# A sparse layer's rotated queries: transposed by TensorE, or by VectorE and a trip through memory

## The chip, the cores and the metric

The kernel runs on one core of a Trainium2 chip. The metric is device time in microseconds (us). Three runs of the kernel before took 723.4, 724.43 and 725.69 us; the median, 724.43 us, is the time before.

## The reference, cut to what matters

The model is a chain of layers over 256 positions of 1024 features, in float32: feed-forward, a mixer, feed-forward, a "forgetting" attention (fox) and a sparse attention (dsa), with the last two followed by a layer norm. The change lies in dsa:

```python
q, ckv, kr, qi, ki, wi, gate = split(x @ w_in)
q = rope(q.reshape(B, S, 8, 128))          # the first 32 of 128 are rotated
q_lat = einsum('bshn,hcn->bshc', q[..., 32:], w_uk)
q_full = concat([q_lat, q[..., :32]])
...                                        # an index picks 64 keys per query
logits = einsum('bqhc,bqkc->bhqk', q_full, selected) * 128 ** -0.5
o = softmax(logits) @ selected[..., :128] @ w_uv
out = (silu(gate) * o) @ w_out
```

## The kernel before, in words

The 256 positions are two tiles of 128, t = 0 and 1. A projection is computed in blocks: for one tile and 512 columns of weights, four units of two 128-row slices. Each float32 weight block is loaded on SyncE's queue (L210), rounded to a high part on ScalarE (`whi`, L197), and its remainder taken on VectorE (`wlo`, L198). Three fp32r matmuls per slice (L164) make one float32 product, so a block of 512 columns is 24 matmuls. `prefetch` runs up to eight units ahead.

In dsa the order of work is: an index block for each tile (`idx`, `idx_T`, `index`, `add`, with the top-k selection on VectorE at L991 and L992), then q in two halves j of four heads, each for t = 0 and 1, then the gate blocks (`attend`: two for tile 0, two for tile 1), between which the scores, softmax, products and `uv` of six groups of heads run, then the output projection (`out_proj`).

For one q block, `q_evac` copies the product out of PSUM on ScalarE (`yq`, L1016) and rotates it with six VectorE instructions (L920 to L925). `go` transposes its four heads on TensorE with the identity (`tr`, L179), copies the result scaled to `qT` (L1024), and puts the 32 rotated rows into `qs`, a stack of high part, remainder and high part again (L1026 to L1028). When both tiles of a half are there, `q_lat` multiplies by `w_uk` (two heads a call), and ScalarE and VectorE evacuate it. The scores use `qlT` and `qs`.

The order of the calls comes from a small planner. `self.now` is advanced by each matmul's planned time alone; `later(us, fn)` puts a call on a heap, due at `now + us`; `when` waits for named events first; `pump`, at the end of each unit, calls what is due; `drain` calls all that is left. The numbers are in `DUE`: `go` follows `q_evac` by `dsa_qT` = 6.31 us, and `q_lat` follows `go` of tile 1 by 1.0 and 2.0 us. This order is a rank and not yet the order on the engines: the framework that builds the program puts each engine's instructions into a fixed order by its own estimate of when inputs are there, and takes the earlier call where several could run. Each engine then runs its list strictly in that order and waits at each instruction for what it needs.

The feed-forward layers already have the other way to transpose: VectorE transposes 32x32 blocks of a 128x512 tile (`hb`, L413), and `regroup` (L275) moves the blocks to their partitions. It writes `hb` to a buffer in memory with four DMAs (L282, 128 KB each) and reads it back with one (L283, 512 KB), all on GpSimd's queue. Then `hh` (L239, ScalarE) and `hl` (L240, VectorE) split the landed `hd`, 9.5 us of planned time after the call.

Of the kernel before, what the change touches and what calls it, by code (L numbers as in the profile page):

```python
# [9 lines left out]
F32 = mybir.dt.float32  # L10
F32R = mybir.dt.float32r
BF16 = mybir.dt.bfloat16
AF = mybir.ActivationFunctionType
# [3 lines left out]
P = 128  # L17
S = 256
D = 1024
# [9 lines left out]
SC128 = 128 ** -0.5  # L29
# [17 lines left out]
def unit_list():  # L47
# [38 lines left out]
DUE = {  # L86
    "ffn_T": 9.5,
    "ffn_x": 3.0,
    "mix_T": 9.32,
    "mix_pool1": 1.21,  # L90
    "mix_pool2": 1.49,
    "mix_s": (0.5, 0.55, 3.0),
    "mix_pv": 1.0,
    "mix_pv2": 4.74,
# [5 lines left out]
    "out_T": 2.04,  # L100
    "dsa_idx": 3.93,
    "dsa_isc": (4.17, 0.39, 10.61),
    "dsa_qT": 6.31,
    "dsa_ql": (1.0, 2.0),
    "dsa_pv2": 1.64,
    "dsa_uv": 10.62,
# [8 lines left out]
class Kern:  # L115
# [40 lines left out]

    def drain(self):
        while self.heap:
            due, _, fn = heapq.heappop(self.heap)
            self.now = max(self.now, due)  # L160
            fn()
# [495 lines left out]
    def silu_gate(self, pool, acc, out, hr):  # L657

        nc = self.nc
        th = pool.tile([P, 512], F32, name="th", bufs=2)  # L660
        nc.scalar.activation(th, acc, AF.Tanh, scale=0.5 if hr is None else hr)
        nc.vector.scalar_tensor_tensor(out, th, 1.0, acc, op0=ALU.add, op1=ALU.mult)

    def out_proj(self, u, after, last=False):

        for t in range(2):
            o = [self.bank("mm") for _ in range(2)]
            for n in range(2):
                if last and t == n == 1:
                    o = [o[0], o[1], self.bank("mm")]  # L670
                    for j, c in enumerate((slice(0, 256), slice(256, 512))):
                        for i in range(4):
                            self.half(o[1 + j], self.xT[t], u + 4 + i, i == 0, i == 3, cols=c)
                    continue
                for i in range(4):
                    self.half(o[n], self.xT[t], u + 4 * n + i, i == 0, i == 3)
                    if t == 1:
                        self.done(u + 4 * n + i + 1)
                    if t == 1 or i % 2:
                        self.prefetch(1)  # L680
            if t == 0:
                self.before_t1()
            after(t, o)
        return u + 8
# [185 lines left out]
    def gate_out(self, t, hb, o, l, f, gt):  # L870

        nc = self.nc
        ri = self.small("ri", 4, bufs=4)
        nc.vector.reciprocal(ri, l[:, 4 * hb:4 * hb + 4])
        nc.vector.tensor_scalar(ri, ri, f, None, op0=ALU.mult)
        for i in range(4):
            c = slice((4 * hb + i) * P, (4 * hb + i + 1) * P)
            nc.vector.scalar_tensor_tensor(gt[:, c], o[:, i * P:(i + 1) * P], ri[:, i:i + 1], gt[:, c],
                                           op0=ALU.mult, op1=ALU.mult)
        self.when([(self.stage, "open", t)], DUE["out_T"], lambda: self.put_T(  # L880
            self.xT[t], t, gt[:, 512 * hb:512 * hb + 512], 4 * hb, 4))


    def dsa(self, u, x_gain=None):
        self.stage = "dsa"
        nc, tc, A = self.nc, self.tc, self.A
        with tc.tile_pool(name="dsa", bufs=1, reuse_waits="tile") as pool:
# [5 lines left out]
            rope = pool.tile([P, 2, 96], F32, name="rope")  # L893
            nc.sync.dma_start(out=rope, in_=A["rope"])
            y = [pool.tile([P, 744], F32, name=f"y{t}", tag=f"A{t}") for t in range(2)]
            gt = [pool.tile([P, D], F32, name=f"g{t}") for t in range(2)]
            kiT, ckvT = (pool.tile([P, P], F32, name=n) for n in ("kiT", "ckvT"))
            qiT = pool.tile([P, 4, P], F32, name="qiT")
            kiTs, ckvTs = (self.parts(pool, [P, S], n) for n in ("kiTs", "ckvTs"))
# [3 lines left out]
            qs = pool.tile([96, 8, S], F32R, name="qs")  # L903
            ckvs = [tuple(pool.tile([P, P], F32R, name=f"ckv{c}{t}") for c in "hl") for t in range(2)]
            ckv = [pool.tile([P, P], F32, name=f"ckv{t}") for t in range(2)]
            qT = [pool.tile([P, 4, S], F32, name=f"qT{j}") for j in range(2)]
# [6 lines left out]
            def do_rope(x, n, half, t, off):  # L913

                x1, x2 = x[:, :, 0:half], x[:, :, half:2 * half]
                bc = lambda o: rope[:, t, None, off + o:off + o + half].to_broadcast([P, n, half])
                m = pool.tile([P, 2, 9 * 8], F32, name="rm", bufs=2)
                m1 = m[:, 0, :n * half].rearrange("p (n d) -> p n d", n=n)
                m2 = m[:, 1, :n * half].rearrange("p (n d) -> p n d", n=n)
                nc.vector.tensor_tensor(m1, x2, bc(half), op=ALU.mult)  # L920
                nc.vector.tensor_tensor(m2, x1, bc(half), op=ALU.mult)
                nc.vector.tensor_tensor(x1, x1, bc(0), op=ALU.mult)
                nc.vector.tensor_tensor(x2, x2, bc(0), op=ALU.mult)
                nc.vector.tensor_tensor(x1, x1, m1, op=ALU.subtract)
                nc.vector.tensor_tensor(x2, x2, m2, op=ALU.add)  # L925
# [88 lines left out]
            def q_evac(acc, t, j):  # L1014
                yq = pool.tile([P, 512], F32, name="yq", bufs=2)
                nc.scalar.copy(yq, acc)  # L1016
                do_rope(yq.rearrange("p (h d) -> p h d", h=4), 4, 16, t, 0)

                def go():
                    ps = self.bank("tr")  # L1020
                    for i in range(4):
                        self.tr(ps[:, i * P:(i + 1) * P], yq[:, i * P:(i + 1) * P])
                    hs, c = slice(4 * j, 4 * j + 4), slice(t * P, (t + 1) * P)
                    nc.scalar.activation(qT[j][:, :, c], ps.rearrange("p (i q) -> p i q", i=4), AF.Copy,  # L1024
                                         scale=SC128)
                    nc.scalar.copy(qs[0:32, hs, c], qT[j][0:32, :, c])  # L1026
                    nc.vector.tensor_sub(qs[32:64, hs, c], qT[j][0:32, :, c], qs[0:32, hs, c].bitcast(F32))
                    nc.scalar.copy(qs[64:96, hs, c], qs[0:32, hs, c].bitcast(F32))  # L1028
                    if t == 1:
                        for g in range(2):  # L1030
                            self.later(DUE["dsa_ql"][g], lambda g=g: q_lat(2 * j + g))
                self.later(DUE["dsa_qT"], go)

            def q_lat(g):
                ps = self.bank("sc").rearrange("p (h k) -> p h k", h=2)
                for i in range(2):
                    self.mm(ps[:, i, :], wuk[:, 2 * g + i, :], qT[g // 2][:, 2 * (g % 2) + i, :], True, True)
                nc.scalar.copy(qlT[:, 2 * g:2 * g + 2, :], ps[:, :, 0:P])
                self.split_psum(*(d[:, 2 * g:2 * g + 2, :] for d in qlTs), ps[:, :, P:S])
                self.fire(("dsa", "ql", g))  # L1040

            for j in range(2):
                for t, acc in self.chunk(u, 4):
                    q_evac(acc, t, j)
                u += 4
# [44 lines left out]
            for t, g in GROUPS:  # L1090
                ql = [("dsa", "ql", i) for i in ((2 * g, 2 * g + 1) if t == 0 else (g,))]
                self.when([("dsa", "sel", t)] + ql, 0.0, lambda t=t, g=g: self.fire(("dsa", "k", t, g)))
            self.attend(u, pool, gt, [None, None], scores, pv)
            u += 8
            rows = []
# [88 lines left out]
def layout(inp):  # L1184
# [7 lines left out]
        "fox": fox, "fox_fv": np.concatenate([fox[:, 3072:3080], fox[:, 2048:3072]], 1),  # L1192
        "fox_out": a["fox_w_out_2"],
        "dsa": dsa, "dsa_idx": np.concatenate([ki, qi, wi, kr, ckv], 1), "dsa_out": a["dsa_w_out_2"],
    }
    for i in (1, 2):
# [38 lines left out]
```

## Time and profile before

| | |
|---|---|
| median of three runs | 724.43 us |
| the profiled execution | 723.93 us, of which the span from first to last instruction is 722.1 |
| TensorE matmul busy | 706.5 us, 98% |
| VectorE busy | 492.1 us, 68% |
| ScalarE busy | 369.4 us, 51% |
| GpSimd busy | 62.3 us, 9% |
| mean granted TensorE clock | 0.993 of full speed |

Busy shares are averages over stages with different limits; the dsa layer begins at about 602 us of the span. Rows of a time line give start, duration, engine, line, operation with its tiles and shapes, a count, and in brackets the idle time of the engine just before and what ended it.

### The profile page before, as it was taken

The page shows a single profiled execution, that of the slowest core. Times are in us where ns is not written, and L with a number is a line of the kernel's source. Part 1 is how long each engine was busy: PE and PEld are TensorE (multiplying, and loading weights), DVE is VectorE, ACT ScalarE, POOL GpSimd, SP SyncE. Part 2 cuts the span into 40 slices and gives each one's busy share as a digit, 9 for nine tenths or more (in the row PEclk, how much of TensorE's full clock was granted, in tenths as well). Part 3 has the DMA queues.
Part 4 walks back from the last instruction along what each step waited for, and adds up shares of the span by engine and source line. Part 5 has one row for each costly group of instructions (what it writes and reads, how often), then busy time and mean ns, then how long its engine had stood idle before and what let it go on. Part 6 is the DMA issues. An engine that isn't in the chain of part 4 may idle for free.

```text
span 722.1 us, 9816 instructions
## 1 busy us (share of the span) xinstructions
PE 706.5 (98%) x3580; PEld 593.9 (82%) x3580; DVE 492.1 (68%) x790; ACT 369.4 (51%) x552; POOL 62.3 (9%) x90
## 2 busy tenths in 40 slices
PE   8999999999999999999999999999999999999995
PEld 7788889888888778888889888778898888778984
DVE  5776765575647867666776575556456968997965
ACT  6654544454545645454454354446464635675820
POOL 0101110300001001011110300000300001000001
PEclk9999999999999999999999999999999999999998
DMA  8898666875734425668765885546572527633501
GB/s 253 305 317 309 212 215 208 285 266 188 271 122 167 154 94 181 202 199 288 228 224 196 270 265 189 196 142 195 169 248 101 156 63 251 206 118 117 175 1 59
DMA packets 42305, 140.87 MB, mean 195 GB/s; under 512 B 5512, under 2 KB 6672, under 8 KB 42128
## 3 DMA queue, kind: packets, MB, share of 16 engines
q1 hardware_dynamic: 37728, 127.23, 52.7%
q0 software_dynamic: 4096, 12.60, 5.1%
q8 instruction: 28, 0.46, 0.2%
q10 hardware_dynamic: 432, 0.41, 0.2%
q14 instruction: 21, 0.17, 0.1%
HBM read 133.39 MB, written 6.82 MB: 194 GB/s over the span
## 4 chain that ended last, share of the span: by engine, by line
PE 88%; DVE 5%; DMA 3%; ACT 2%; issue 1%; SPq 0%; POOL 0%; DVEq 0%; POOLq 0%; ACTq 0%
PE mm L164 79%; PE sc L164 5%; PE tr L179 3%; DVE wlo L198 2%; DMA raw<-in_w 1%; DMA row_final_norm<-in_final_norm 1%; PE tr L164 1%; ACT whi L197 1%; DMA xin<-in_xT 1%; ACT s L445 0%; DVE sel L983 0%; DVE xl L317 0%; DVE sel L992 0%; DVE s L534 0%; POOL hrs L292 0%
## 5 line engine op out<-in xcount | busy, mean ns | idle before, releaser
L198 DVE TENSOR_TENSOR wlo<-raw,whi 128x1024 fp32r<-128x1024 f32 (+3 forms) x236 | 274.6, 1178 | 84.8 <-ACT whi L197 74.9
L197 ACT CAST whi<-raw 128x1024 fp32r<-128x1024 f32 (+3 forms) x236 | 235.7, 1014 | 126.0 <-PE mm L164 76.4
L164 PE MATMUL mm<-whi,xh 128*128 128x512 f32 (+3 forms) x760 | 289.3, 381 | 1.7 <-ACT whi L197 1.6
L164 PE MATMUL mm<-whi,xl 128*128 128x512 f32 (+3 forms) x760 | 284.9, 375 | 2.2 <-DVE xl L246 2.2
L164 PE MATMUL mm<-wlo,xh 128*128 128x512 f32 (+3 forms) x760 | 284.0, 375 | 0.1
L164 PEld LDWEIGHTS mm<-whi,xh 128*128 128x128 f32 x760 | 144.0, 189 | 25.7 <-ACT whi L197 3.0
L164 PEld LDWEIGHTS mm<-whi,xl 128*128 128x128 f32 x760 | 144.2, 190 | 25.0 <-DVE xl L246 2.7
L164 PEld LDWEIGHTS mm<-wlo,xh 128*128 128x128 f32 x760 | 143.9, 189 | 25.3 <-DVE wlo L198 1.3
L164 PE MATMUL mm<-whi,hh 128*128 128x512 f32 x176 | 68.7, 390 | 0.0
L164 PE MATMUL mm<-whi,hl 128*128 128x512 f32 x176 | 68.5, 389 | 0.0
L164 PE MATMUL mm<-wlo,hh 128*128 128x512 f32 x176 | 68.5, 389 | 0.0
L240 DVE TENSOR_TENSOR hl<-hd,hh 128x512 fp32r<-128x512 f32 (+1 forms) x24 | 14.5, 644 | 53.3 <-ACT hh L239 53.3
L239 ACT CAST hh<-hd 128x512 fp32r<-128x512 f32 (+1 forms) x24 | 12.8, 583 | 60.9 <-DMA hd<-d 60.9
L282 POOL DMA_DIRECT2D d<-hb x48 | 26.5, 559 | 149.9 <-DVE hb L413 136.3
L164 PEld LDWEIGHTS mm<-wlo,hh 128*128 128x128 f32 x176 | 33.0, 188 | 6.9
L164 PEld LDWEIGHTS mm<-whi,hh 128*128 128x128 f32 x176 | 33.1, 188 | 6.7
L164 PEld LDWEIGHTS mm<-whi,hl 128*128 128x128 f32 x176 | 33.1, 188 | 6.7
L400 ACT ACTIVATE th<-mm,hr 128x512 f32<-128x512 f32 (+1 forms) x24 | 15.6, 648 | 25.2 <-PE mm L164 24.1
L445 ACT ACTIVATE s<-s,nmax 128x128 f32<-128x128 f32 (+1 forms) x48 | 21.3, 446 | 7.0 <-DVE nmax L443 7.0
L292 POOL TENSOR_TENSOR rs<-ms,mhalf 128x1 f32<-128x1 f32 x10 | 6.5, 653 | 175.4 <-DVE ms L305 175.4
L402 DVE SCALAR_TENSOR_TENSOR a<-th,mm 128x512 f32<-128x512 f32 (+1 forms) x24 | 15.2, 632 | 8.5 <-ACT th L400 8.5
L292 POOL TENSOR_TENSOR lr<-ve,mhalf 128x1 f32<-128x1 f32 x4 | 4.0, 992 | 167.8 <-DVE ve L640 167.8
(219 smaller groups left out, 602.0 us busy)
## 6 DMA issues: line engine op xcount, KB each, us to landing
raw<-in_w SPq DMA_DIRECT2D x208, 512.0 KB, 4.5
d<-hb POOLq DMA_DIRECT2D x40, 128.0 KB, 4.8
hd<-d POOLq DMA_DIRECT2D x10, 512.0 KB, 6.6
raw<-in_w SPq DMA_DIRECT2D x12, 344.0 KB, 3.6
raw<-in_w SPq DMA_DIRECT2D x8, 372.0 KB, 3.6
raw<-in_w SPq DMA_DIRECT2D x8, 256.0 KB, 4.4
x<-in_x SPq DMA_DIRECT2D x2, 512.0 KB, 6.3
B<-in_bias SPq DMA_DIRECT2D x1, 1024.0 KB, 7.0
```

What stands on the lines that cost most here:

```text
L164: self.nc.tensor.matmul(out, a, b, start=start, stop=stop)
L179: self.nc.tensor.transpose(out, a, self.ident[:p, :p])
L197: nc.scalar.copy(hi[:, :m], raw[:, :m])
L198: nc.vector.tensor_sub(lo[:, :m], raw[:, :m], hi[:, :m].bitcast(F32))
L239: nc.scalar.copy(hi, src)
L240: nc.vector.tensor_sub(lo, src, hi.bitcast(F32))
L282: self.nc.gpsimd.dma_start(out=d[a].rearrange("b i m -> i b m"), in_=src[32 * a:32 * a + 32])
L292: self.nc.gpsimd.tensor_tensor(out, a, self.mhalf[:, 0:1].to_broadcast(list(a.shape)), op=ALU.pow)
L400: nc.scalar.activation(th[:, :w], acc[:, :w], AF.Tanh, scale=hr[t])
L402: nc.vector.scalar_tensor_tensor(a[t][:, :w], th[:, :w], 1.0, acc[:, :w], op0=ALU.add, op1=ALU.mult)
L445: nc.scalar.activation(s[:, h, :], s[:, h, :], AF.Exp, bias=m[:, h:h + 1], accum_out=l[:, col + h:col + h + 1])
```

## The change

The rotated q is no longer transposed by TensorE. VectorE transposes each rotated block in 32x32 blocks into `qb`; when both tiles of a half are in, `regroup` sends them through memory into `qd`. `go`, now once a half and due 9.0 us after the second tile, copies `qd` to `qT` and `qs` as before. `qb` has one buffer and shares it with the gate of tile 1 (`g1`, made later), and `th` of the gate shares the buffers of `yq`. `out_proj` first runs the planner until the transposes of the gated output of its tile have been called; this also holds for fox.

```diff
-    "dsa_qT": 6.31,
+    "dsa_qT": 9.0,
...
+    def until(self, keys):
+
+        while not all(k in self.fired for k in keys):
             due, _, fn = heapq.heappop(self.heap)
             self.now = max(self.now, due)
             fn()
...
-        th = pool.tile([P, 512], F32, name="th", bufs=2)
+        th = pool.tile([P, 512], F32, name="th", tag="yq" if self.stage == "dsa" else "th", bufs=2)
...
         for t in range(2):
+            self.until([(self.stage, "og", t, hb) for hb in range(2)])
             o = [self.bank("mm") for _ in range(2)]
...
-        self.when([(self.stage, "open", t)], DUE["out_T"], lambda: self.put_T(
-            self.xT[t], t, gt[:, 512 * hb:512 * hb + 512], 4 * hb, 4))
+
+        def go():
+            self.put_T(self.xT[t], t, gt[:, 512 * hb:512 * hb + 512], 4 * hb, 4)
+            self.fire((self.stage, "og", t, hb))
+        self.when([(self.stage, "open", t)], DUE["out_T"], go)
...
-            gt = [pool.tile([P, D], F32, name=f"g{t}") for t in range(2)]
+            gt = [pool.tile([P, D], F32, name=f"g{t}") for t in range(1)]
...
                 do_rope(yq.rearrange("p (h d) -> p h d", h=4), 4, 16, t, 0)
 
+                if t == 0:
+                    self.qb = pool.tile([P, 4, 256], F32, name="qb", tag="g1")
+                nc.vector.transpose(self.qb[:, :, t * P:(t + 1) * P].rearrange("p b (c j) -> p b c j", c=4),
+                                    yq.rearrange("p (c b j) -> p b c j", c=4, b=4))
+                if t == 0:
+                    return
+                qd = pool.tile([P, 4, 256], F32, name="qd")
+                self.regroup(qd, self.qb)
+
                 def go():
-                    ps = self.bank("tr")
-                    for i in range(4):
-                        self.tr(ps[:, i * P:(i + 1) * P], yq[:, i * P:(i + 1) * P])
-                    hs, c = slice(4 * j, 4 * j + 4), slice(t * P, (t + 1) * P)
-                    nc.scalar.activation(qT[j][:, :, c], ps.rearrange("p (i q) -> p i q", i=4), AF.Copy,
-                                         scale=SC128)
-                    ...
+                    hs = slice(4 * j, 4 * j + 4)
+                    for tt in range(2):
+                        c = slice(tt * P, (tt + 1) * P)
+                        nc.scalar.activation(qT[j][:, :, c].rearrange("p c (a j) -> p c a j", a=4),
+                                             qd[:, :, c].rearrange("p a (c j) -> p c a j", c=4), AF.Copy, scale=SC128)
+                        nc.scalar.copy(qs[0:32, hs, c], qT[j][0:32, :, c])
+                        nc.vector.tensor_sub(qs[32:64, hs, c], qT[j][0:32, :, c], qs[0:32, hs, c].bitcast(F32))
+                        nc.scalar.copy(qs[64:96, hs, c], qs[0:32, hs, c].bitcast(F32))
+                    for g in range(2):
+                        self.later(DUE["dsa_ql"][g], lambda g=g: q_lat(2 * j + g))
                 self.later(DUE["dsa_qT"], go)
...
+            gt.append(pool.tile([P, D], F32, name="g1", tag="g1"))
             self.attend(u, pool, gt, [None, None], scores, pv)
```

## Rows read from the trace of the kernel before

**Rows 1.** The page's chain that ended last, shares of the span by engine.
```profile
PE 88%; DVE 5%; DMA 3%; ACT 2%; issue 1%; SPq 0%; POOL 0%; DVEq 0%; POOLq 0%; ACTq 0%
```
**Rows 2.** The chain in order of time: start, us, what.
```profile
514.09 5.49 PE mm L164 x24
...
640.43 0.44 PE tr L179 x4
...
642.26 1.73 PE sc L164 x8
...
699.75 13.94 PE mm L164 x84
```
**Rows 3.** Stretches: length, busy us of PE, PEld, DVE, ACT, POOL, clock, DMA share, GB/s.
```profile
655.00:660.00 5.00, 5.00 (x33) 4.44 (x31) 4.93 (x14) 1.40 (x3) 0.00 (x0) 1.00 0.38 139
660.00:665.00 5.00, 5.00 (x32) 4.20 (x31) 2.85 (x7) 4.28 (x15) 0.00 (x0) 1.00 0.08 30
```
**Rows 4.** Time line of TensorE, the first transposes of yq.
```profile
633.84 0.63 PE L179 MATMUL tr<-cst,yq 128*128 128x128 f32 x4 [0.25 <-DVE yq L925]
```
**Rows 5.** Time line of VectorE in the feed-forward layers.
```profile
59.71 0.71 DVE L413 STREAM_TRANSPOSE hb<-h 128x512 f32<-128x512 f32 x1
...
73.74 1.30 DVE L240 TENSOR_TENSOR hl<-hd,hh 128x512 fp32r<-128x512 f32 x2 [6.19 <-ACT hh L239]
74.95 0.74 DVE L411 SCALAR_TENSOR_TENSOR h<-a,qr,mm 128x512 f32<-128x512 f32 x1
...
372.63 0.71 DVE L413 STREAM_TRANSPOSE hb<-h 128x512 f32<-128x512 f32 x1
```
**Rows 6.** Time line of GpSimd: a regroup of a feed-forward layer, and 704 us.
```profile
60.72 2.19 POOL L282 DMA_DIRECT2D d<-hb  x4 [17.25 <-DVE hb L413]
68.01 0.76 POOL L283 DMA_DIRECT2D hd<-d  x1 [5.10 <-DMA d<-hb]
...
704.45 0.99 POOL L292 TENSOR_TENSOR lr<-ve,mhalf 128x1 f32<-128x1 f32 x1 [76.01 <-DVE ve L640]
```
**Rows 7.** Time line of ScalarE in the feed-forward layers.
```profile
58.72 0.69 ACT L400 ACTIVATE th<-mm,hr 128x512 f32<-128x512 f32 x1 [0.81 <-PE mm L164]
...
73.08 1.14 ACT L239 CAST hh<-hd 128x512 fp32r<-128x512 f32 x2 [6.80 <-DMA hd<-d]
...
387.39 1.14 ACT L239 CAST hh<-hd 128x512 fp32r<-128x512 f32 x2 [7.44 <-DMA hd<-d]
```
**Rows 8.** Time line of VectorE: last instructions of three rotations, and a subtraction.
```profile
637.19 0.68 DVE L1027 TENSOR_TENSOR qs<-qT,qs 32x512 fp32r<-32x512 f32 x1
...
638.98 0.22 DVE L924 TENSOR_TENSOR yq<-yq,rm 128x64 f32<-128x64 f32 x1
...
645.93 0.22 DVE L925 TENSOR_TENSOR yq<-yq,rm 128x64 f32<-128x64 f32 x1
...
655.98 0.22 DVE L925 TENSOR_TENSOR yq<-yq,rm 128x64 f32<-128x64 f32 x1
```
**Rows 9.** Time line of ScalarE: the last q evacuation, and copies to qT and qs.
```profile
649.36 0.57 ACT L1016 COPY yq<-mm 128x512 f32<-128x512 f32 x1
...
657.18 0.60 ACT L1024 ACTIVATE qT<-tr 128x512 f32<-128x512 f32 x1 [2.51 <-PE tr L179]
657.81 0.62 ACT L1026 CAST qs<-qT 32x512 fp32r<-32x512 f32 x1
```
**Rows 10.** Time line of TensorE: transposes of two neighbouring calls of `idx_T`.
```profile
613.43 0.27 PE L179 MATMUL tr<-cst,ckv 128*128 128x128 f32 x1
...
615.57 0.28 PE L179 MATMUL tr<-cst,y 128*32 128x128 f32 x1
```
**Rows 11.** Time line of TensorE at the start of the fox layer.
```profile
470.49 0.80 PE L164 MATMUL mm<-whi,xl 128*128 128x512 f32 x1 [2.23 <-DVE xl L246]
```
**Rows 12.** Stretches of one microsecond behind that wait.
```profile
470.00:471.00 1.00, 0.52 (x1) 0.50 (x2) 1.00 (x2) 0.00 (x0) 0.00 (x0) 0.66 0.46 184
...
473.00:474.00 1.00, 1.00 (x4) 0.77 (x4) 1.00 (x3) 0.00 (x0) 0.00 (x0) 0.63 0.82 324
```

More of the change, by code (lines that the diff above doesn't have):

```diff
@@ L158, in drain @@
         while self.heap:
+            due, _, fn = heapq.heappop(self.heap)
+            self.now = max(self.now, due)
+            fn()
+    def until(self, keys):
+        while not all(k in self.fired for k in keys):
             due, _, fn = heapq.heappop(self.heap)
@@ L1017, in q_evac @@
                 do_rope(yq.rearrange("p (h d) -> p h d", h=4), 4, 16, t, 0)
-                def go():
-                    ps = self.bank("tr")
-                    for i in range(4):
-                        self.tr(ps[:, i * P:(i + 1) * P], yq[:, i * P:(i + 1) * P])
-                    hs, c = slice(4 * j, 4 * j + 4), slice(t * P, (t + 1) * P)
-                    nc.scalar.activation(qT[j][:, :, c], ps.rearrange("p (i q) -> p i q", i=4), AF.Copy,
-                                         scale=SC128)
[L1026 to L1031, printed above, removed]
+                if t == 0:
[6 more added lines that the diff above has]
+                self.regroup(qd, self.qb)
+                def go():
+                    hs = slice(4 * j, 4 * j + 4)
[8 more added lines that the diff above has]
+                        self.later(DUE["dsa_ql"][g], lambda g=g: q_lat(2 * j + g))
                 self.later(DUE["dsa_qT"], go)
```

## The prediction

> **What bounds the kernel now.** I read the profile's own chain of waits first. It runs 88% over TensorE [rows 1]: matmuls and what feeds them decide the end. The piece that matters here is the last 90 us. From the transposes at 633.84 us [rows 4] on, the chain never leaves TensorE until the last 84 matmuls of the output projection, 699.75 + 13.94 = 713.7 us [rows 2]. So in this stretch one microsecond of TensorE work removed is one microsecond of the kernel, and one microsecond for which TensorE waits is lost. Next I read busy time by stretch: VectorE is as good as full until 660 us (4.93 of 5) and has room after it (2.85 of 5) [rows 3]. It runs the top-k selection there, whose result is needed only by later scores, so it is full but not the bound.
>
> **What is removed.** Sixteen transposes of yq in four groups. In the chain a group is 0.44 us [rows 2], and the first group waited 0.25 us for the rotation on VectorE [rows 4]. Gain on the bounding engine: 4 x 0.44 + 0.25 = 2.0 us. It is certain as work; what can undo it is waiting. The `tr` bank is also freed, and no row shows TensorE waiting for one; I take nothing.
>
> **What is added off the path.**
> - VectorE gets four 32x32 block transposes of 128x512, 0.71 us each in the feed-forward layer [rows 5]: 2.8 us on a nearly full engine. Cover: three of the four subtractions of line 1027, 0.68 us each [rows 8], now come after 655 us, so the load before 660 us stays about the same. Without that cover the second tile's selection, and the scores behind it, come 2.8 us later. Work is only added, so nothing lies below 0; bounds 0 and 2.8, taken 0.
> - GpSimd issues ten DMAs in two sets of 2.19 + 0.76 us [rows 6]. Before its next instruction, at 704.45 us, it idled for 76.01 us, so nothing else is queued there; the weight queue on SyncE is another one and is not passed. The 2 MB that this moves fall where the DMA engines are 0.38 and 0.08 busy [rows 3]. Taken 0.
> - `qb` has one buffer. The block transpose of tile 0 of the second half must wait until the first half's four DMAs have read it. In the feed-forward layer the second leg was issued 68.01 - 60.42 = 7.6 us after the last transpose [rows 5, 6]; here that is 639.9 + 7.6 = 647.5 us, while that rotation ends at 646.15 us [rows 8]. VectorE waits 1.4 us with wlo and the selection queued behind it. Weights are split up to eight blocks ahead and the selection is used ten microseconds later, so 0 on the path, 1.4 as the other end.
> - ScalarE copies from SBUF instead of PSUM. The sequence qT, qs, qs, qT is 0.60 + 0.62 + 0.62 + 0.60 = 2.44 us for a half [rows 9]; before, each tile's copies stood alone. This goes into the latency below.
> - `until` in the output projection only moves calls ahead. In the forgetting layer both keys fire soon after the gates of tile 0, two gate blocks before the projection, so it does nothing. In the sparse layer it ranks `uv` and the transposes of the gated output above the projection's blocks. The shared th/yq buffers are free after a block transpose, well before th needs them at 654 us. 0 for all three.
>
> **What is added on the path: latency.** The old way from rotation to the q_lat matmuls took under 3 us. The new one goes VectorE, four DMAs, memory, one DMA, ScalarE. The feed-forward layer does exactly this with the same shapes. From the end of the last transpose to the first copy of the landed data: 73.08 - 60.42 = 12.66 us, and 387.39 - 373.34 = 14.05 [rows 5, 7].
> First half: the rotation of tile 1 ends at 639.20 us [rows 8], the transpose at 639.9, data are there at 652.6 to 654.0, and with 2.44 us of copies q_lat can start at 655.0 to 656.4 us. It started at 642.26 [rows 2].
> Is TensorE busy until then? The last q block ended at 649.4 us (its evacuation in [rows 9]); without three transpose groups (1.6) and with the eight q_lat matmuls (1.73 in [rows 2]) behind it it ends at 646.1. Two gate blocks of 5.49 us [rows 2] follow, to 657.1. There is just enough work to hide it, if the instruction order puts q_lat behind that work.
> I think it does not. q_lat is called 10 and 11 us of planned matmul time after the last q evacuation of its half, and two q blocks are 11 us: the call ranks ahead of the gate blocks. The engines do not follow the calls; they run what the program builder thought ready. Of two neighbouring calls, the transposes of ckv and of kr, one runs at 613.43 and one at 615.57 us, with twelve matmuls of another block between [rows 10]. So q_lat stands where the builder expected the data. How wrong is its idea of this regroup? In the feed-forward layer th of tile 0 was released by TensorE at 58.7 us [rows 7], so the next two blocks end at 58.7 + 2 x 5.49 = 69.7 us and h (line 411) could have run. But hl stands before it in VectorE's order, and VectorE idled 6.19 us until 73.74 [rows 5]. The order thus expected hl by 69.7 and hh 0.66 earlier, 69.0, which is 8.6 us after the transpose against 12.66 measured: about 4.0 us too early, and up to 6.8 us, the whole of ScalarE's wait [rows 7]. There it cost nothing, since TensorE had other blocks. Here TensorE itself stands at q_lat, its order is fixed, and the rest of the gate blocks are behind it. Bounds 0 to 6.8; taken 4.0, the nearest row in shape and size.
>
> **The clock.** After a wait of 2.23 us TensorE came back at half clock [rows 11]: 0.66, 0.50, 0.50, 0.63 in the four microseconds from 470 us, of which the first and last are [rows 12]. That is 0.34 + 0.50 + 0.50 + 0.37 = 1.7 us lost. A 4 us wait is longer, so I add 1.7; bounds 0 and 3.4 (two such waits). The Trainium skill ("TensorE: Matmul & The Clock Gate", section on the HAM clock gate) says an idle array falls to 1.2 GHz and must earn 2.4 GHz back; by that rule, which speaks against this change, the trace agrees with 0.50 behind the wait.
>
> **Second half.** The rotation of its tile 1 ends at 656.2 us [rows 8]; transposed 656.9, landed 669.6 to 671.0, copied 672.0 to 673.4. From 646.1 TensorE has 11.0 (gates of tile 0) + 1.7 (q_lat) + 5.7 (wait and clock) + 11.0 (gates of tile 1) = 29.4 us, to 675.5, before it must have these data, and the first scores besides. The order is again 4 us early, but TensorE already runs 4 us late. Taken 0. The other end is 4.0: if VectorE stands at a subtraction that waits for the first regroup, with the last rotation queued behind, the second chain slips too.
>
> **Sum.** -2.0 + 4.0 + 1.7 = +3.7 us on the profiled execution's 723.93 us, 727.6. That execution is 0.5 us under the median of the runs, so 728.1 us for the median.
>
> **Rivals.**
> - *The gate blocks cover the chain* (faster). The place is q_lat of the first half; it decides if it stands after 655 us in TensorE's order. For: 11 us of gate work, by row just enough. Against: the calls rank ahead of it and the order was 4 us early for the same chain. Price: no wait, no clock loss, -2.0: 722.4 us. The Trainium skill ("DMA: Bandwidth & Descriptors", section on the anatomy of one DMA) gives about 2.0 us plus bytes over 436 GB/s; an estimate by that page is 2.3 and 3.2 us for the two legs, 8.8 us with issuing, no wait and this case's time. The rows have 12.66 and 14.05 us, so I do not follow it.
> - *A short wait eats the gain.* The DMA engines are nearly idle here [rows 3]; if the chain is 2 us shorter for it, TensorE waits 2 us, which is just under the 2.23 us of [rows 11], and keeps its clock: -2.0 + 2.0 = 0, 724.4 us. Against: neither chain read is that short.
> - *Both halves wait*: 6.8 for the first, 4.0 for the second, 1.7 of clock, -2.0: +10.5, 734.9 us. For: ScalarE's waits of 6.8 us and VectorE's full queue. Against: the gate blocks of tile 1 cover the second.
>
> **How the numbers follow.** Forecast 0.45, its own range 725.5 to 731; cover 0.27; short wait 0.12; both halves 0.16. Some 0.3% (2.2 us) is what a measurement can tell. Cover straddles that bound at 722.3: 0.19 faster, 0.08 the same. With the short wait and 0.02 of the forecast the same gets 0.22, and slower 0.59. The range takes cover and both halves in: 721.5 to 735.0.
>
> **What would show it.** No yq transposes on TensorE, 2 us less of `tr`. Regroups of 12 to 14 us on GpSimd's queue. ScalarE's qT waiting for a DMA and TensorE waiting 4 us at the first q_lat with a clock near 0.5 behind. I am wrong if q_lat stands behind both gate blocks without a wait, if the regroup takes under 9 us, or if the wait is at scores or at VectorE instead.

## The result, and the profile after

The changed kernel takes 728.53 us (median of seven runs, 727.18 to 729.97); the kernel before, run beside it, 723.4. The ratio is 1.0064, 95% interval 1.0041 to 1.0087: slower by 4.6 us (5.1 between the two medians), where 3.7 was forecast. The profiled execution is 729.09 us with a span of 727.3.

TensorE timeline of the kernel after: the two q_lat groups and the later waits (start, duration, line, tiles, count, idle before and its end).

```profile
657.21 1.99 PE L171 MATMUL sc<-qT,wuk 128*128 128x256 f32 x8 [2.91 <-ACT qT L1043]
...
668.71 1.89 PE L171 MATMUL sc<-qT,wuk 128*128 128x256 f32 x8
...
686.82 0.63 PE L186 MATMUL tr<-cst,s 128*128 128x128 f32 x4 [0.59 <-DVE pTl L247]
...
689.19 1.16 PE L171 MATMUL sc<-wuv,ol 128*128 128x128 f32 x8 [0.27 <-ACT ol L1098]
691.02 0.38 PE L171 MATMUL sc<-pTh,ckvl 128*128 128x256 f32 x1 [0.68 <-ACT ol L1098]
```

The first q_lat waits 2.91 us for ScalarE's copy of the regrouped data; before, TensorE had one wait of 0.25 us in the whole stretch behind 630 us [rows 4]. The second q_lat doesn't wait. Then, thirty microseconds behind the first wait, TensorE waits for the products of the softmax. Busy time by stretch (TensorE, its weight loads, VectorE, ScalarE, GpSimd, granted clock, DMA share, GB/s):

```profile
655.00:660.00 5.00, 2.79 (x13) 2.41 (x14) 4.90 (x11) 3.94 (x9) 2.18 (x4) 1.00 0.63 145
...
685.00:690.00 5.00, 3.93 (x25) 2.95 (x25) 5.00 (x6) 4.63 (x8) 0.00 (x0) 1.00 0.05 18
690.00:695.00 5.00, 4.33 (x33) 3.67 (x32) 3.98 (x16) 1.76 (x3) 0.00 (x0) 1.00 0.01 3
```

TensorE is idle for 2.2 us in the window of the first q_lat (its wait began before 655 us) and for 1.7 us between 685 and 695 us; until 690 us VectorE (5.00 of 5) and ScalarE (4.63) are the full ones there. The clock stays at 1.00 all through. The regroups on GpSimd's queue:

```profile
642.19 2.25 POOL L289 DMA_DIRECT2D d<-qb  x4 [12.64 <-DVE qb L1032]
651.42 0.78 POOL L290 DMA_DIRECT2D qd<-d  x1 [6.98 <-issue]
655.43 2.18 POOL L289 DMA_DIRECT2D d<-qb  x4 [3.22 <-DVE m L1002]
662.06 0.76 POOL L290 DMA_DIRECT2D qd<-d  x1 [4.45 <-DMA d<-qb]
```

VectorE, the block transpose that completes the first half, and the second half's last rotation and transposes:

```profile
641.19 0.71 DVE L1032 STREAM_TRANSPOSE qb<-yq 128x512 f32<-128x512 f32 x1
...
650.45 0.22 DVE L931 TENSOR_TENSOR rm<-yq,rope 128x64 f32<-128x64 f32 x1 [0.94 <-ACT yq L1027]
...
651.98 0.70 DVE L1032 STREAM_TRANSPOSE qb<-yq 128x512 f32<-128x512 f32 x1
...
654.42 0.70 DVE L1032 STREAM_TRANSPOSE qb<-yq 128x512 f32<-128x512 f32 x1
```

ScalarE, the copies of the regrouped halves:

```profile
656.01 1.15 ACT L1043 ACTIVATE qT<-qd 128x512 f32<-128x512 f32 x2 [2.62 <-DMA qd<-d]
...
667.26 1.15 ACT L1043 ACTIVATE qT<-qd 128x512 f32<-128x512 f32 x2
```

From the end of the last block transpose of a half to the first copy is 656.01 - 641.90 = 14.1 us and 667.26 - 655.12 = 12.1 us; the feed-forward layer's chains were 12.66 and 14.05 [rows 5, 7]. Last, the end of the chain of waits (start, duration, what, count):

```profile
701.36 0.44 PE tr L186 x4
701.80 17.84 PE mm L171 x101
```

Behind the last transposes of the gated output 101 matmuls of the output projection are left, 17.84 us; before it were 84 and 13.94 us [rows 2]. More of the projection is left when attention is through.

The profiled executions differ by some 5 us in when the sparse layer begins, so below its times count from the `lr` of the layer norm ahead of it (L292 before, L299 after; 602.96 and 603.74 us). All columns but the ratio are from the profiled executions. The last column is TensorE's idle time from 45 us of the layer to its last matmul and, behind the plus, what the granted clock took there (the length of a stretch times the missing share of the clock).

| kernel | ratio, 95% interval | wait at 1st, 2nd q_lat | 2nd q_lat starts | matmuls behind last transposes | last matmul ends | TensorE idle + clock |
|---|---|---|---|---|---|---|
| before | 1 | 0, 0 | 55.4 | 84 | 110.7 | 0 |
| after | 1.0064, 1.0041 to 1.0087 | 2.91, 0 | 65.0 | 101 | 115.9 | 4.9 |
| side_edits | 0.9996, 0.9971 to 1.0020 | 0, 0 | 55.6 | 90 | 111.1 | 0 |
| dead_regroup | 1.0031, 1.0011 to 1.0051 | 0, 1.18 | 55.8 | 90 | 112.9 | 1.6 |
| half0_memory | 1.0036, 1.0017 to 1.0054 | 0.68, 0.43 | 58.8 | 90 | 114.2 | 3.4 |
| half1_memory | 1.0073, 1.0046 to 1.0100 | 0, 1.31 | 68.8 | 101 | 118.1 | 3.2 |
| no_memory | 1.0011, 0.9994 to 1.0028 | 0, 0 | 59.0 | 99 | 113.1 | 1.8 |
| no_transposes | 1.0204, 1.0176 to 1.0232 | 7.43, 0.34 | 77.5 | 101 | 127.2 | 12.0 + 5.1 |
| sp_queue | 1.0058, 1.0037 to 1.0080 | 0, 0 | 65.5 | 101 | 116.4 | 3.6 + 1.7 |
| act_queue | 1.0125, 1.0099 to 1.0152 | 0, 0 | 70.5 | 101 | 120.6 | 6.0 + 1.7 |
| late_qlat | 1.0022, 1.0005 to 1.0039 | 0, 0 | 64.9 | 91 | 112.3 | 0.3 |
| later_selection | 1.0060, 1.0034 to 1.0085 | 2.94, 0 | 67.2 | 101 | 117.6 | 3.8 + 1.7 |
| no_memory_relief | 1.0048, 1.0030 to 1.0067 | 0, 0 | 59.6 | 99 | 114.7 | 3.0 |
| three_edits | 1.0062, 1.0036 to 1.0088 | 0, 0 | 64.9 | 101 | 114.8 | 4.1 |

One of the ten runs of later_selection, 784.49 us at a granted clock of 0.849, is left out of its ratio.

The last column for the kernels before and after, as the windows show it (length, then busy time of TensorE, its weight loads, VectorE, ScalarE, GpSimd, clock, DMA share, GB/s):

```profile
647.96:713.67 65.71, 65.71 (x391) 57.63 (x389) 50.19 (x102) 31.19 (x70) 0.99 (x1) 1.00 0.26 89
...
648.74:719.63 70.89, 65.98 (x379) 55.86 (x377) 52.34 (x111) 34.92 (x80) 4.71 (x7) 1.00 0.33 104
```

Before, TensorE has no idle time in this stretch. After, it has 4.9 us: 2.9 at the first q_lat and 2.0 behind the second.

### The profile page after: what moved, and what is told of

Read it like the earlier page. It is cut to its first block, busy times and chain, and to the rows that moved or that the text cites. A ratio compares the mean times of both kernels' runs of the same rounds, so it can differ in the third digit from the quotient of the medians.

```text
span 727.3 us, 9810 instructions
## 1 busy us (share of the span) xinstructions
PE 707.1 (97%) x3564; PEld 592.7 (81%) x3564; DVE 493.3 (68%) x794; ACT 367.1 (50%) x552; POOL 68.0 (9%) x100
## 5 line engine op out<-in xcount | busy, mean ns | idle before, releaser
L246 ACT CAST hh<-hd 128x512 fp32r<-128x512 f32 (+1 forms) x24 | 12.8, 582 | 67.2 <-DMA hd<-d 67.2
L407 ACT ACTIVATE th<-mm,hr 128x512 f32<-128x512 f32 (+1 forms) x24 | 15.6, 648 | 15.2 <-PE mm L171 14.1
L299 POOL TENSOR_TENSOR rs<-ms,mhalf 128x1 f32<-128x1 f32 x10 | 6.5, 651 | 172.7 <-DVE ms L312 172.7
L418 DVE SCALAR_TENSOR_TENSOR h<-a,qr,mm 128x512 f32<-128x512 f32 (+1 forms) x24 | 16.7, 695 | 2.3 <-PE mm L171 2.3
```

Source lines behind the costliest of these rows:

```text
L246: nc.scalar.copy(hi, src)
L299: self.nc.gpsimd.tensor_tensor(out, a, self.mhalf[:, 0:1].to_broadcast(list(a.shape)), op=ALU.pow)
L407: nc.scalar.activation(th[:, :w], acc[:, :w], AF.Tanh, scale=hr[t])
L418: nc.vector.scalar_tensor_tensor(h[:, :w], a[t][:, :w], qr[t], acc[:, :w], op0=ALU.mult, op1=ALU.mult)
```

## The experiments

Theory A: the loss is TensorE's wait for the regrouped data at q_lat. Rival B: the side edits. Rival C: VectorE's added work. Rival D, formed on the trace after: the score groups that come late bunch up behind the last matmuls that could stand beside them.

**side_edits.** The old `go` with its transposes on TensorE; kept are `until`, the th/yq buffers and the late `g1`.

```diff
-    "dsa_qT": 9.0,
+    "dsa_qT": 6.31,
...
-                qd = pool.tile([P, 4, 256], F32, name="qd")
-                self.regroup(qd, self.qb)
...
+                    for i in range(4):
+                        self.tr(ps[:, i * P:(i + 1) * P], yq[:, i * P:(i + 1) * P])
```

> The change without its core: TensorE transposes yq again, due 6.31 us as before; kept are `until`, the th/yq buffers and the late g1. Theory A (the regroup's latency is the loss: TensorE waits at q_lat and the late scores wait behind it): as before, ratio 0.999 to 1.002, no wait over 1 us at q_lat. Rival B (the side edits, or the order that they change ahead of and behind dsa, cost it): ratio 1.004 or more. The whole change has 1.0064.

0.9996, with no wait at q_lat. B is out.

**dead_regroup.** side_edits plus the transposes and regroups, unread.

```diff
+                nc.vector.transpose(self.qb[:, :, t * P:(t + 1) * P].rearrange("p b (c j) -> p b c j", c=4),
+                                    yq.rearrange("p (c b j) -> p b c j", c=4, b=4))
+                if t == 1:
+                    qd = pool.tile([P, 4, 256], F32, name="qd")
+                    self.regroup(qd, self.qb)
```

> The kernel of side_edits plus the four VectorE block transposes and both regroups through memory, whose result nothing reads. Theory A: the added work alone is hidden, ratio 0.999 to 1.002. Rival C (VectorE's 2.8 us of transposes, or the DMA traffic beside the weights, delays the selection and the weight remainders): ratio 1.003 to 1.006, with TensorE waiting for wlo or at the scores of tile 1.

1.0031: C has a part, 2.2 us (0.8 to 3.7). TensorE's timeline in this kernel shows where:

```profile
656.72 0.63 PE L186 MATMUL tr<-cst,yq 128*128 128x128 f32 x4 [0.40 <-DVE yq L936]
...
661.22 1.13 PE L171 MATMUL sc<-qT,wuk 128*128 128x256 f32 x4 [1.18 <-DVE s L1078]
```

VectorE is full up to 660 us, so its 2.8 us more make the last rotation late and the first scores' evacuation; q_lat waits until they are out of PSUM. "Full but not the bound" was too kind: it had no slack left. The DMA traffic is not parted from the transposes here; no_memory below has the transposes without it, and about as much idle time on TensorE (1.8 us for 1.6).

**half0_memory, half1_memory.** One half by the new way, the other by TensorE (`go_te` is the old `go`). The first diff is for half0_memory; half1_memory has `j == 0`.

```diff
+                if j == 1:
+                    self.later(6.31, go_te)
+                    return
                 if t == 0:
                     self.qb = pool.tile([P, 4, 256], F32, name="qb", tag="g1")
```

> Only the first half j = 0 goes through memory; TensorE transposes the second half. Theory A: half the saving (1.0 us), but TensorE still waits at the first half's q_lat, 2 to 4 us, and the scores come late: ratio 1.001 to 1.005. Rival C (added work, same for either half): half of the loss, 1.003, as for the other half. Rival D (it is the second half's late scores that cost): ratio 0.998 to 1.000.

> Only the second half j = 1 goes through memory; TensorE transposes the first half. Theory A as the wait at the first q_lat alone: that wait is gone, half the saving is left, ratio 0.998 to 1.000. Rival D (the second half's q_lat comes so late that the last four score groups bunch up behind it): ratio 1.002 to 1.005 with TensorE waiting behind 670 us. Rival C: 1.003.

The first half alone costs 1.0036 and the second alone 1.0073, as much as the whole change; together they are more than the change, and why was not looked for. For half0_memory D's range (0.998 to 1.000) fails. A's range holds the number, but the wait that A names, 2 to 4 us at q_lat, is 0.68. The longest wait is at the other half's transposes, whose rotation is late on VectorE:

```profile
654.97 0.63 PE L186 MATMUL tr<-cst,yq 128*128 128x128 f32 x4 [1.66 <-DVE yq L936]
656.74 1.99 PE L171 MATMUL sc<-qT,wuk 128*128 128x256 f32 x8 [0.68 <-ACT qT L1059]
```

In half1_memory the first q_lat doesn't wait at all and starts 41.2 us into the layer (39.1 before). The second stands where only 21 gate matmuls are left:

```profile
671.93 1.99 PE L171 MATMUL sc<-qT,wuk 128*128 128x256 f32 x8 [1.31 <-ACT qT L1059]
...
692.57 0.39 PE L171 MATMUL sc<-pTh,ckvl 128*128 128x256 f32 x1 [0.94 <-ACT ol L1114]
```

A as the first q_lat's wait predicted 0.998 to 1.000 here and falls; D's 1.002 to 1.005 is the nearer. (About 2 us of this profile's lateness arise before the change's place, at 610 to 620 us, where TensorE waits and its clock falls; without them its last matmul is still 5.3 us later than before. The ratio comes from all runs.)

**no_memory.** ScalarE reads `qb`, no DMA.

```diff
-                qd = pool.tile([P, 4, 256], F32, name="qd")
-                self.regroup(qd, self.qb)
+                qd = self.qb
```

> The whole change without the trip: ScalarE reads qT from qb at once, and the regroup's DMAs are left out (the blocks stay on their partitions, so the queries are mixed up). VectorE's transposes stay. Theory A (latency of the trip is the loss): TensorE never waits at q_lat and the saved transposes show, ratio 0.997 to 0.999. Rival C (VectorE's 2.8 us on a full engine, as the unread transposes and regroups cost 1.0031): 1.001 to 1.003 with waits for VectorE's selection, scores or rotation.

1.0011: A's range is missed, and C's holds it at its lower end, with the wait for VectorE that C named. It is 0.5% under the change, with intervals that do not meet: the trip is worth about 3.8 us, and what is left, 0.8 us, is a saving eaten by waits such as this one on TensorE:

```profile
659.57 0.50 PE L171 MATMUL mm<-wlo,xh 128*128 128x512 f32 x1 [1.30 <-DVE wlo L205]
```

If the saved transposes are worth 1.5 us (four groups, each 0.37 us from start to next start), VectorE's work costs 0.8 + 1.5 = 2.3 us here, about the 2.2 of dead_regroup.

**no_transposes.** ScalarE copies the projection into `qb`, which is rotated there and regrouped; `th` has buffers of its own again.

```diff
-                yq = pool.tile([P, 512], F32, name="yq", bufs=2)
-                nc.scalar.copy(yq, acc)
-                do_rope(yq.rearrange("p (h d) -> p h d", h=4), 4, 16, t, 0)
+                yq = self.qb[:, :, t * P:(t + 1) * P]
+                nc.scalar.copy(yq, acc.rearrange("p (h d) -> p h d", h=4))
+                do_rope(yq, 4, 16, t, 0)
```

> The whole change without VectorE's block transposes: the rotated q is written into qb directly and regrouped as it is (the blocks are not transposed, so the queries are mixed up). The trip stays. Theory A: the wait at the first q_lat stays or grows, since q_lat now stands behind 50 instead of 60 matmuls: 2.9 + 2.3 - 0.7 = 4.5 us, ratio 1.006 to 1.010. Rival C: without VectorE's 2.8 us the kernel falls to 1.000 to 1.004.

1.0204, outside both. It is no clean test: without `yq`, the second half's evacuation itself waits for the one `qb` to be read, and the second q_lat comes 12.5 us later than in the change. The first q_lat waits 7.43 us, and the clock falls behind it:

```profile
655.00:660.00 5.00, 0.00 (x0) 0.00 (x0) 2.67 (x14) 0.00 (x0) 0.00 (x0) 0.71 0.63 218
660.00:665.00 5.00, 2.82 (x7) 2.28 (x8) 2.23 (x6) 3.96 (x8) 0.00 (x0) 0.50 0.01 2
```

**sp_queue.** The regroups are issued by SyncE.

```diff
-                self.regroup(qd, self.qb)
+                self.regroup(qd, self.qb, nc.sync)
```

> The whole change with the regroup's DMAs on SyncE's queue, between the weight loads, instead of GpSimd's. The instruction order has the first q_lat behind 69 matmuls instead of 60, 2.0 us later. Theory A: if the trip takes no longer, the wait at the first q_lat falls from 2.9 us to under 1, ratio 1.002 to 1.005; if SyncE is held by a weight buffer, the trip is later by that and the ratio is over 1.007. Rival D (the score groups that bunch up behind the second q_lat are the loss): 1.005 to 1.008 without a long wait at q_lat.

This speaks against A as the price. SyncE's queue holds the regroups up by nothing that shows:

```profile
638.20 2.22 SPq L290 DMA_DIRECT2D d<-qb  x4
640.53 3.77 SPq L217 DMA_DIRECT2D raw<-in_w  x2
644.63 0.38 SPq L291 DMA_DIRECT2D qd<-d  x1
650.38 1.79 SPq L290 DMA_DIRECT2D d<-qb  x4
```

The first trip takes 650.00 - 638.16 = 11.8 us (ScalarE's first copy, the end of the transpose), no q_lat waits, and the kernel is still 1.0058, in D's range (the interval reaches into A's). TensorE's waits and the stretches in which the later ones fall:

```profile
651.84 0.50 PE L171 MATMUL mm<-wlo,xh 128*128 128x512 f32 x1 [0.82 <-DVE wlo L205]
...
681.66 0.98 PE L171 MATMUL sc<-pTh,ckvl 128*128 128x256 f32 x2 [1.28 <-ACT pTh L246]
687.93 0.39 PE L171 MATMUL sc<-pTh,ckvl 128*128 128x256 f32 x1 [0.68 <-ACT ol L1099]
```

```profile
680.00:685.00 5.00, 3.62 (x19) 2.65 (x18) 5.00 (x7) 4.55 (x12) 0.00 (x0) 0.86 0.21 69
685.00:690.00 5.00, 4.32 (x30) 4.13 (x29) 2.75 (x12) 1.23 (x3) 0.00 (x0) 0.80 0.02 3
```

The wait at the first q_lat is gone, and TensorE loses as much elsewhere: it waits for VectorE's weight remainder near the same place, and longer at the softmax's end (2.3 us from 78 us of the layer on, 1.75 in the change). Here the clock does fall: 5 x (0.14 + 0.20) = 1.7 us. Without that fall this profile would show less loss than the change's; that the price stays rests on the ratio of all runs.

**act_queue.** The same, with ScalarE as issuer (`nc.scalar`).

> The whole change with the regroup's DMAs issued by ScalarE instead of GpSimd. The first q_lat stands behind 63 matmuls instead of 60. Theory A: issuing is quicker than GpSimd's 2.25 us for four plus the 2.0 us pause before the read, so the data land 2 to 4 us earlier and the wait at the first q_lat is under 1 us: ratio 1.001 to 1.004. Rival D: 1.005 to 1.008, TensorE waiting behind 680 us for ol, pTl or s.

1.0125. No q_lat waits, but ScalarE must stand until the four writes have landed before it can issue the read, with its copies queued behind:

```profile
649.46 0.59 ACT L1028 COPY yq<-mm 128x512 f32<-128x512 f32 x1 [3.25 <-DMA d<-qb]
```

That copy comes only 0.6 us later in the layer than in the change. But the order of VectorE's list is another one here: steps of the selection stand ahead of the last rotation, which starts 4 us after the copy's end.

```profile
654.12 0.22 DVE L932 TENSOR_TENSOR rm<-yq,rope 128x64 f32<-128x64 f32 x1
```

So the second half's transposes end later (659.46 us) and its q_lat starts at 70.5. The expectation had the trip right (652.88 - 641.68 = 11.2 us for the first half) and missed what the new order does to the second half.

**late_qlat.** side_edits with q_lat called later.

```diff
-    "dsa_ql": (1.0, 2.0),
+    "dsa_ql": (12.0, 13.0),
```

> The kernel of side_edits (TensorE transposes, no trip, no VectorE transposes) with q_lat alone called 11 us of planned time later: the first q_lat stands behind 60 matmuls of the last q block and the gates, as after the change, the second behind 96 (94 after the change); their data are long there. Theory A (the wait for landed data is the loss): no wait at q_lat, ratio 0.999 to 1.001. Theory D (scores, softmax and products that come after the gate blocks run out have no matmuls beside them, whatever made them late): ratio 1.002 to 1.006, TensorE waiting behind the last gate block.

1.0022: lateness by itself, with no trip, no VectorE work and no wait at q_lat, costs 1.6 us (0.4 to 2.8). The interval touches the upper end of A's range and holds the lower half of D's. But TensorE doesn't wait behind the last gate block, as D had it, though the second q_lat starts as late as in the change (64.9). In the trace the two q_lats stand behind 54 and 90 matmuls, six and four fewer than in the change (60 and 94). TensorE has only 0.3 us of idle time, so the profile shows no wait for the 1.6 us. By this run, the place of q_lat in the order is the smaller part of the 4.6 us.

**later_selection.** The whole change with the selection of tile 1 called later.

```diff
-    "dsa_isc": (4.17, 0.39, 10.61),
+    "dsa_isc": (4.17, 0.39, 14.0),
```

> The whole change, with the second call of the index of tile 1 due 14.0 instead of 10.61 us, so that its selection on VectorE stands less in front of the second half's rotation and transposes. The second q_lat moves from 94 to 90 matmuls and the scores of tile 1 up by about as many. Theory D with VectorE's order as the cause of the second half's lateness: 1 to 2 us better than the change, ratio 1.003 to 1.005. Theory A: the first q_lat stands where it stood, ratio 1.006.

1.006, no gain, as A said; the interval reaches into the range of D with VectorE's order as the cause (from 1.0034), but nothing here speaks for it. The second q_lat moved up in the order and yet started later, at 67.2: the first one starts 1.6 us later than in the change for waits ahead of it, waits as long as there, and this time the clock falls.

```profile
657.88 3.68 PE L171 MATMUL sc<-qT,wuk 128*128 128x256 f32 x8 [2.94 <-ACT qT L1043]
```

```profile
655.00:660.00 5.00, 2.12 (x5) 1.75 (x6) 4.93 (x13) 3.30 (x6) 2.18 (x4) 0.80 0.61 142
660.00:665.00 5.00, 5.00 (x26) 4.24 (x26) 4.74 (x15) 1.30 (x5) 0.76 (x1) 0.86 0.50 147
```

**no_memory_relief.** no_memory with the subtractions of `qs` on GpSimd.

```diff
-                        nc.vector.tensor_sub(qs[32:64, hs, c], qT[j][0:32, :, c], qs[0:32, hs, c].bitcast(F32))
+                        nc.gpsimd.tensor_sub(qs[32:64, hs, c], qT[j][0:32, :, c], qs[0:32, hs, c].bitcast(F32))
```

> The kernel of no_memory (no trip, queries mixed up) with the four subtractions of qs, 0.68 us each, on GpSimd instead of VectorE. Theory C (VectorE's added 2.8 us cost 2.3 us: no_memory has 1.0011 where 0.998 is left without them): VectorE has as much as before, ratio 0.997 to 0.999. If the waits in no_memory have another cause: 1.001.

1.0048, slower than no_memory, with intervals that do not meet: VectorE was not relieved. GpSimd's subtractions and VectorE's instructions beside them:

```profile
636.89 1.54 POOL L1045 TENSOR_TENSOR qs<-qT,qs 32x512 fp32r<-32x512 f32 x1 [7.84 <-issue]
644.69 1.56 POOL L1045 TENSOR_TENSOR qs<-qT,qs 32x512 fp32r<-32x512 f32 x1 [6.25 <-ACT qs L1044]
650.59 1.29 POOL L1045 TENSOR_TENSOR qs<-qT,qs 32x512 fp32r<-32x512 f32 x1 [4.34 <-ACT qs L1044]
```

```profile
637.21 2.31 DVE L205 TENSOR_TENSOR wlo<-raw,whi 128x1024 fp32r<-128x1024 f32 x1
...
645.03 1.30 DVE L933 TENSOR_TENSOR yq<-yq,rope 128x64 f32<-128x64 f32 x1
...
650.95 0.41 DVE L1003 MATCH_REPLACE8 sel<-m,sel 128x256 f32<-128x256 f32 x1
```

A wlo takes 1.21 us on average in no_memory, and the other three rotations of line 933 take 0.21 here. Both instructions have grown by 1.1 us; the replacement at 650.95, beside the third subtraction, has not (0.41). The Trainium skill ("SBUF — State Buffer", section "SBUF: two separate sides") says that a VectorE instruction with two SBUF inputs and a GpSimd instruction that reads SBUF exclude each other for whole instructions; the rows of the two grown instructions agree. Of what was taken off VectorE, 4 x 0.68 us, these two stops alone gave back 2.2 us, and TensorE's idle time rose from 1.8 to 3.0 us, so C is neither confirmed nor refuted by this run.

**three_edits.** sp_queue, the subtractions on GpSimd and the later selection together.

> The whole change with three edits: regroups on SyncE's queue, the subtractions of qs on GpSimd, the later selection. Theories C and D: the wait at the first q_lat is gone and VectorE is relieved, but the trip still pushes scores behind the gate blocks: ratio 1.000 to 1.004. Theory A: all of the loss is gone, 0.997 to 0.999, faster than the kernel before.

1.0062, above the ranges of all three theories (the interval, from 1.0036, reaches into that of C and D). A falls again: no q_lat waits, and nothing is won. But the run before shows that the subtractions on GpSimd cost 2.7 us by themselves, so this kernel doesn't tell what the other two edits are worth without them. Near the place of the first q_lat TensorE waits for VectorE:

```profile
656.95 0.49 PE L171 MATMUL sc<-ckvT,qlT 128*128 128x128 f32 x2 [1.32 <-DVE qlTsl L247]
```

So in no_memory, sp_queue and three_edits, where the first q_lat doesn't wait, TensorE waits 0.8 to 1.3 us for VectorE between 51.7 and 56.5 us of the layer, near the place where the change waits for the trip (53.5). In the change VectorE works on during those 2.9 us, so a part of that wait may hide a delay that would have come anyway; this was not tested. No kernel tried beats the kernel before.

## Why the prediction was right in its sum and wrong in its place

- **Removed TensorE work, -2.0.** 1.5 us between starts, plus the 0.25 us wait: near enough, 0.25 us too much.
- **The trip, 12.66 to 14.05 us.** 14.1 and 12.1 measured. The 8.8 us estimated from the Trainium skill ("DMA: Bandwidth & Descriptors", anatomy of one DMA) was too short; on SyncE's queue it was 11.8.
- **TensorE waits at the first q_lat, +4.0.** The mechanism is there, 2.91 us, in the place named (12 matmuls into the second gate block, data about 3 us after their place in the order). But it is not the price: sp_queue has no such wait and loses about as much (three_edits too, with the subtractions on GpSimd in it).
- **Half clock behind it, +1.7.** Didn't happen; the clock was 1.00. It happened in later_selection behind a wait of 2.94 us, so the length of the wait alone did not decide it.
- **Second half, taken 0.** This is the step that failed. It was right that TensorE doesn't wait at the second q_lat, and wrong to stop there. half1_memory, where only this half makes the trip, costs 1.0073 by itself. In the change its data land 63.5 us into the layer, q_lat starts at 65.0 instead of 55.4, scores, softmax, products, `uv` and gating of three of the six groups follow it, and TensorE waits 2.0 us behind it. The 9.6 us of lateness are not all loss: 34 more matmuls of the last q block and the gates stand ahead of this q_lat (94 for 60), and behind it TensorE needs 48.9 us without its waits, for 55.3 before. That takes up 6.4 us; 3.2 us are lost by then, the wait at the first q_lat above all, and 2.0 behind it, together the 5.2 us by which the last matmul is later. In the seven kernels where the second half makes the trip, the last matmul ends 49.3 to 50.9 us after the second q_lat, at 64.9 as at 77.5. Most of that is TensorE's own work left behind it, so the regularity alone shows no chain of waits: late_qlat, with the copies of qT and qs done early, ends 47.4 us after it with next to no idle time.
- **VectorE's transposes, 0 of 0 to 2.8.** 2.2 and 2.3 us in the two kernels where TensorE doesn't wait for the trip. In both, three (dead_regroup) or two (no_memory) of the four subtractions of `qs` still come before 655 us; in the change all four come behind 658, which was the cover argued, so the cost within the change may be less. VectorE is still 4.90 of 5 busy from 655 to 660 us. The second half's last block ends in PSUM near 646 us, as predicted, but is copied only at 649.84, behind a weight cast of ScalarE that itself waited for its load, and transposed by 655.1, between steps of the selection:

```profile
648.88 1.05 ACT L204 CAST whi<-raw 128x1024 fp32r<-128x1024 f32 x1 [1.65 <-DMA raw<-in_w]
```

- **The one buffer `qb`, 0 of 0 to 1.4.** Right as far as the trace shows: VectorE's only wait around the block transpose that needs it is 0.94 us, for the copy out of PSUM.
- **`until`, the buffers, 0.** Right: 0.9996.
- **Rivals.** "Cover" and "short wait" looked at the first q_lat only; the first would have been 722.4 with no wait, and sp_queue has no wait and 1.0058. "Both halves wait" was right that the second half costs something, and put it in the wrong place: a wait at its q_lat, where TensorE waits behind it.

By the terms of the prediction, the change's own trace has -1.5 for -2.0, 2.9 for 4.0, 0 for 1.7, and 2.0 behind the second half for 0. These make 3.4 of the 5.2 us by which the last matmul is later; the rest the profile doesn't show as waits of TensorE. That 3.7 was forecast and 4.6 came is thus partly luck: a clock loss that didn't come and a wait taken too long made up for a price taken as nothing.

From the ratios: the trip 3.8 us; VectorE about 2.3, if the saving is -1.5. They add up to 4.6 because the 2.3 is what no_memory leaves over; only dead_regroup's 2.2 is a second measurement of it. Of the trip's 3.8 us, some 1.6 may come with late q_lat alone. How the other 2 divide between ScalarE's copies and weight casts, now beside the softmax, and the later landing was not separated. Theory D names the place that half1_memory and sp_queue show, but its ranges failed in half0_memory and act_queue, and late_qlat has its lateness without its waits: it is a part of the account and not the whole.

## What to carry to other kernels

When work on the bounding engine is traded for latency, don't ask only whether the consumer waits: follow the consumer's own chain to the end of the kernel, and count what independent work is left to stand beside it. Taking away the first visible wait (another queue) gave 1.0058 for 1.0064, no gain that can be told from noise, so a wait in a trace is priced by removing it and not by its length. VectorE at 4.9 of 5 had no room for 2.8 us more (dead_regroup, 1.0031), though TensorE bounds the kernel.

## What the runs showed of the hardware

- TensorE, idle for 2.91 us, kept a granted clock of 1.00 (after), while 2.94 us of idling (later_selection) had 0.80 and 0.86 in the windows around it, and eight q_lat matmuls took 3.68 us for 1.99. Before, a clock of 0.63 to 0.66 stands behind 2.23 us of idling [rows 11, 12].
- A subtraction of 32x512 is 0.68 us on VectorE and 1.28 to 1.56 us on GpSimd, and two VectorE instructions with two SBUF inputs took about 1.1 us longer beside it (no_memory_relief).
- Four DMAs of 128 KB are issued in 2.18 to 2.25 us by GpSimd and 1.79 to 2.41 by SyncE and ScalarE; the read behind them takes 0.76 to 0.78 us of GpSimd and 0.38 of SyncE. The first half's trip was 14.1 us by GpSimd, 11.8 by SyncE and 11.2 by ScalarE.
- ScalarE as issuer stops at a DMA that depends on another: 3.25 us in its own queue (act_queue).
